# Two squared-ReLU layers on one core: seven block products for eight in the up-projection of 12 of 16 column groups, and weight sums formed by adding DMA transfers

## The chip, the core and the metric

One core of one Trainium2 chip runs the whole program. The metric is device time in microseconds (us), from the start to the end of one execution; the time of the kernel before is the median of three runs. The program is one launch, and all arithmetic is on the core. TensorE is called PE here, VectorE DVE, ScalarE ACT, GpSimd POOL and SyncE SP.

## The reference, cut to what matters

A trunk of two residual layers over 512 tokens of width 1024. Layer 0 mixes tokens by chunked softmax attention, layer 1 by a recurrent block; each is followed by the same kind of dense layer, and only these two dense layers ("MLP 0" and "MLP 1") are changed:

```python
def sq_relu_mlp(h, w1, w2):
    z = jax.nn.relu(jnp.einsum('bsd,df->bsf', h, w1))     # w1: 1024 x 4096
    return jnp.einsum('bsf,fd->bsd', z * z, w2)           # w2: 4096 x 1024
...
        h = h + sq_relu_mlp(rmsnorm(h, norm_mlp[layer]), mlp_w1[layer], mlp_w2[layer])
```

Inputs and output are float32. The RMS norm's per-token factor commutes with relu up to a square, so the kernel feeds `h * gain` into the up-projection and multiplies the squared per-token factor into the down-projection's result.

## The kernel before

**Three matmuls for one product.** Every fp32 operand X is split into a rounded part XH (type fp32r) and a rest XL = X - XH. `mm3` (L217) computes each product as WH·XH + WH·XL + WL·XH, three PE instructions into one PSUM bank. Activations are split once (ACT copies, DVE subtracts); weights are split as they arrive.

**Weights.** `plan` is a list of weight units of 512 KB (128 partitions x 1024 fp32), in the order in which PE uses them. `fetch` (L101) takes the next unit: SP issues its load, ACT casts the high part (L141), DVE subtracts to get the low part (L144). Raw tiles are `wr` (three buffers) or, for the down-projection, the eight tiles `b`; split tiles come from `wsp` (five pairs `wh`, `wl`) and in the MLPs from `wx` too (two more). `want` (L153) hands the next unit to PE after calling `prefetch`, which keeps `state["ahead"]` units fetched: five in the MLPs. The order in which the code emits instructions isn't quite the order in which each queue holds them: a planner of the framework orders each engine's and each DMA queue's instructions by when it expects them to be ready.

**An MLP** (`mlp`, L611) runs in four rounds p over 1024 of the 4096 hidden columns, with the model's width cut into eight blocks of 128 rows.

- *Up-projection*: `up(p, j)` (L649) computes 128 hidden columns for all 512 tokens: 8 row blocks x 3 = 24 matmuls with a 128x128 weight block loaded and 512 tokens moving. ACT applies relu (L656) and square (L657) from PSUM into the tile `a`. Eight units a round: a *group* of four units makes 512 hidden columns, two groups a round, 16 groups in the two MLPs.
- *Down-projection*: `round_(p)` (L669) cuts the 1024 x 512 activations and the 1024 x 1024 block of w2 into 2 x 2 blocks and forms the product with seven block products for eight (the Winograd form of Strassen's algorithm). The sums of activation blocks s1 to s4 (L687 and L731 to L734) are made by DVE, and so are the sums of weight blocks t1 to t4: `V.tensor_sub` in `fetch` (L139), in place in the tiles `b`. Each block product (`product`, L697) takes two weight units and 24 matmuls of 512 moving columns; `read` (L642) adds a PSUM bank, times the per-token factor, into the result.
- The first four up units of round p+1 stand between the block products of round p (`ahead`, L710), the other four open round p+1.
- In round 0 of an MLP, `turn` (L626) transposes the residual by DVE and 32 small DMAs, and `squares` forms the norm's sums.

PSUM holds four banks for up units (`mm`) and four for `X` and `Y` (`at`). GpSimd issues no DMA in this kernel.

The plan of one round in the kernel before, p < 3:

```python
for j in range(4, 8):
    up_(p, j)                       # after the last: "11", two halves
for n, kind in enumerate(("21", "t1", "22", "t2", "t3", "t4"), 1):
    ...                             # two halves each
    if p < 3 and 2 <= n <= 5:
        up_(p + 1, n - 2)
```

Of the kernel before, what the change touches and what calls it, by code (L numbers as in the profile page):

```python
# [15 lines left out]
P = 128  # L16
T = 512
# [23 lines left out]
def trunk(ctx: ExitStack, tc: tile.TileContext, xT, cols, gfin, win, wqkv, wo, rwin, rga, rgx, rwo, w1, w2, out):  # L41
# [4 lines left out]
    wraw = ctx.enter_context(tc.tile_pool(name="wraw", bufs=3))  # L46
# [13 lines left out]
    hT, hT2 = [], []  # L60


    def residual(name):
        both = [per.tile([P, 4, T], F32, name=f"{name}{i}", tag=f"hx{i}") for i in range(2)]
        hT[:] = [both[k // 4][:, k % 4] for k in range(KT)]
        hT2[:] = [both[k // 2][:, 2 * (k % 2) : 2 * (k % 2) + 2] for k in range(4)]
# [9 lines left out]
    rq = per.tile([P, 4], F32, name="rq")  # L76
    fs = per.tile([P, 8], F32, name="fs")
# [20 lines left out]
    state = {"next": 0, "ready": [], "ahead": 4, "stop": None, "more": None, "end": 0, "units": 0}  # L98
    raws, start_ = {}, []

    def fetch():  # L101
        i = state["next"]
        state["next"] += 1
        kind, nk, srcs = plan[i]
        pool = wsp
        if state["more"] is not None and i < state["end"]:
            pool = state["more"] if state["units"] % 7 >= 5 else wsp
            state["units"] += 1
        H = pool.tile([P, 1024], F32R, name=f"wh{i}", tag="wh")
        L = pool.tile([P, 1024], F32R, name=f"wl{i}", tag="wl")  # L110
        n = 1024
        if kind == "plain":
            n = nk * sum(src.shape[1] for src in srcs)
            raw = wraw.tile([P, 1024], F32, name=f"wr{i}", tag="wr")
            rv = raw[:, :n].rearrange("p (k c) -> p k c", k=nk)
            c0 = 0
            for n_, src in enumerate(srcs):
                w = src.shape[1]
                queue = nc.scalar if i == 0 and n_ else nc.sync
                queue.dma_start(rv[:, :, c0 : c0 + w], src.rearrange("(k p) c -> p k c", p=P))  # L120
                c0 += w
        else:
            half, nk = nk, 2
            if kind == "11" and half == 0:
                for name, src in zip(("11", "21", "12", "22"), srcs):
                    both = state["raw"].tile([P, 2, 1024], F32, name=f"b{name}_{i}", tag=f"b{name}")
                    for h in range(2):
                        raws[name, h] = both[:, h]
                        nc.sync.dma_start(
                            raws[name, h].rearrange("p (k c) -> p k c", k=2),  # L130
                            src[h * U : (h + 1) * U].rearrange("(k p) c -> p k c", p=P),
                        )

            at_, x, y = {
                "t1": ("12", "12", "11"), "t2": ("22", "22", "12"), "t3": ("11", "22", "11"), "t4": ("21", "21", "22"),
            }.get(kind, (kind, None, None))
            raw = raws[at_, half]
            if x:
                V.tensor_sub(raw, raws[x, half], raws[y, half])  # L139
# [40 lines left out]
    def add_mlp(layer):  # L180
# [5 lines left out]
        for j in range(4):  # L186
            up_(0, j)
        for p in range(4):
            srcs = [
                w2[layer][(2 * p + k) * T : (2 * p + k + 1) * T, c * T : (c + 1) * T]  # L190
                for k, c in ((0, 0), (1, 0), (0, 1), (1, 1))
            ]
            for j in range(4, 8):
                up_(p, j)
                if j == (5 if p == 3 else 7):
                    plan.extend(("11", half, srcs) for half in range(2))
            for n, kind in enumerate(("21", "t1", "22", "t2", "t3", "t4"), 1):
                for half in range(2):
                    plan.append((kind, half, srcs))
                if p < 3 and 2 <= n <= 5:  # L200
                    up_(p + 1, n - 2)
# [30 lines left out]
    class Norm:  # L232
# [8 lines left out]
        def square(self, k):  # L241
            if self.acc is None:
                self.both = wk.tile([P, 2, T], F32, name=f"{self.name}acc", tag="nn")
# [38 lines left out]
        def spread(self):  # L282
# [3 lines left out]
            r = wk.tile([P, 4, 4, 32], F32, name=f"{self.name}r", tag="nn")  # L286
# [9 lines left out]
    with ExitStack() as actx:  # L296
        ab = actx.enter_context(tc.tile_pool(name="ab", bufs=1))
# [313 lines left out]
    def mlp(ly, norm):  # L611
        with ExitStack() as mctx:
            sr, zp, dp = (mctx.enter_context(tc.tile_pool(name=f"{n}{ly}", bufs=1)) for n in ("sr", "z", "d"))
            wx = mctx.enter_context(tc.tile_pool(name=f"wx{ly}", bufs=2))
            end = starts[ly + 1] if ly + 1 < len(starts) else None
            state.update(raw=sr, more=wx, end=starts[ly] + 4 * 22, units=0, ahead=5, stop=end + 4 if end else None)
            xs = [(hnH[k], hnL[k]) for k in range(KT)]
            res = dp.tile([P, 4, 2, T], F32, name=f"d{ly}", tag="d")
            dt = {(t, c): res[:, t, c] for t in range(4) for c in range(2)}

# [21 lines left out]
            def read(acc, t, c):  # L642
                d, r = dt[t, c], rq[:, t : t + 1]
# [5 lines left out]
            def up(p, j):  # L649
                if j % 4 == 0:  # L650
                    a[p, j // 4] = zp.tile([P, 2, 4, U], F32, name=f"a{ly}{p}{j}", tag=f"a{j // 4}")
# [3 lines left out]
                c = a[p, j // 4][:, :, j % 4, :]  # L655
                S.activation(c, acc.rearrange("p (h c) -> p h c", h=2), AF.Relu)  # L656
                S.activation(c, c, AF.Square)  # L657
                if (p, j) == (0, 0):
                    turn()
                if (p, j) == (0, 5):  # L660
# [3 lines left out]
                if (p, j) == (0, 6):  # L664
                    V.tensor_add(rq, fs[:, 0:8:2], fs[:, 1:8:2])
                    V.tensor_scalar(rq, rq, 1.0 / D, EPS, ALU.mult, ALU.add)
                    V.reciprocal(rq, rq)

            def round_(p):  # L669
                A, low, raw = {}, {}, {}  # L670

                def room(n, kind, tag):
                    return (wk if tag == "nn" else zp).tile([P, 4, U], kind, name=f"{tag}{n}{ly}{p}", tag=tag)

                def place(n, h, l):
                    low[n] = (room(n, F32R, h), room(n, F32R, l))

                def split(n, ks=slice(0, 4)):
                    H, L = low[n]
                    S.copy(H[:, ks], raw[n][:, ks])  # L680
                    V.tensor_sub(L[:, ks], raw[n][:, ks], f(H[:, ks]))

                first, second = a[p, 0], None
                raw["11"], raw["s1"] = first[:, 0], first[:, 1]
                for n, tag in (("s3", "c"), ("s2", "f"), ("s4", "g")):
                    raw[n] = room(n, F32, tag)
                ins = V.tensor_sub(raw["s3"], raw["11"], raw["s1"])  # L687
                if (ly, p) == (0, 1):
                    constants(ins)
                place("11", "h0", "l")  # L690
                split("11")
                place("12", "h1", "nn")
                Y, X = ([atp(f"{b}{ly}{p}{t}") for t in range(2)] for b in "yx")
                Z = [mmp(f"z{ly}{p}{t}") for t in range(2)]
# [15 lines left out]
                def ahead(j):  # L710
                    if p < 3:
                        up(p + 1, j)


                def step(name, bank, fresh, t0, c):
                    apart = p == 3 and name != "12"
                    if not apart:
                        product(name, bank, fresh)
                    for t in range(2):
                        if apart:  # L720
                            product(name, bank, fresh, ts=(t,))
                        read(bank[t], t0 + t, c)

                chunks = {5: slice(0, 2), 7: slice(2, 4)} if p < 3 else {5: slice(0, 2), 6: slice(2, 3), 7: slice(3, 4)}
                for j in range(4, 8):
                    up(p, j)
                    raw["12"], raw["22"] = a[p, 1][:, 0], a[p, 1][:, 1]
                    if j in chunks:
                        ks = chunks[j]
                        r = {n: raw[n][:, ks] for n in raw}  # L730
                        V.tensor_sub(r["s2"], r["22"], r["s3"])  # L731
                        V.tensor_sub(r["s4"], r["12"], r["s2"])
                        split("12", ks)
                        V.tensor_add(r["s1"], r["s1"], r["22"])  # L734

                    if j == (5 if p == 3 else 7):
                        step("11", X, True, 0, 0)


                place("s1", "h0", "l")  # L740
                split("s1")
                step("12", Z, True, 0, 0)
                place("s4", "h1", "nn")
                split("s4")
                if p == 3:
                    state["ahead"] = 3
                step("s1", Y, True, 2, 1)
                place("s2", "h2", "g")
                split("s2")
                place("s3", "h0", "f")  # L750
                split("s3")
                ahead(0)
                step("s4", Y, False, 0, 1)
                place("22", "h1", "c")
                split("22")
                ahead(1)
                step("s2", X, False, 0, 1)
                ahead(2)
                if p == 3:

                    (ends if ly else turns)(step, product, X)
                    return
                step("s3", X, False, 2, 1)
                ahead(3)
                step("22", X, False, 2, 0)

# [9 lines left out]
            def turns(step, product, X):  # L776
                banks = [atp(f"back{i}") for i in range(2)]
# [305 lines left out]
```

## Time and profile before

| | |
|---|---|
| median of 3 runs | 1053.45 us (1053.26 to 1053.67) |
| profiled execution, device time | 1053.21 us |
| its span in the trace | 1051.4 us |
| mean granted PE clock | 0.998 of full speed |
| MLP 0, MLP 1 in the span | about 245 to 572 us, about 719 to 1045 us |
| up-projection matmuls, both MLPs | 3 x 512, each with 512 moving columns |
| bytes moved by DMA | 115.71 MB |

Times in the profile are microseconds from the start of the span unless ns stands beside them. A row of the groups gives the line of the code, the engine, the operation, its output and inputs by name, the shape and the count, then the busy time in all and the mean ns of one. Matmul records overlap (one is shown as 390 ns long, while the next one starts earlier), so the cost of a matmul in a train is the distance between two starts. A row of windows gives, for a stretch of time, the busy time and the count of instructions of each engine (PE, PEld, DVE, ACT, POOL), the granted clock, the share of time in which the 16 DMA engines were busy, and GB/s.

### The profile page before, as it was taken

The numbers are of one execution on the slowest core, as the hardware profiler recorded it, in microseconds if no ns is written. First come the engines' busy times: TensorE is split into PE (matmuls) and PEld (weight loads), VectorE is DVE, ScalarE is ACT, GpSimd is POOL, SyncE is SP. The second block draws the span as 40 slices with busy tenths as digits, with TensorE's granted clock in tenths as the row PEclk, the third lists the DMA queues.
The fourth block names the chain that finished last, engine by engine and source line by source line (L and its number), as shares of the span: only waits on it lengthen the run. The fifth ranks groups of instructions, "written<-read, shape, count | busy, mean of one in ns | idle before, by whom it ended". The sixth has DMA issues, their size and how long they took to land.

```text
span 1051.4 us, 12857 instructions
## 1 busy us (share of the span) xinstructions
PE 1042.3 (99%) x4754; PEld 865.5 (82%) x4754; DVE 807.2 (77%) x1202; ACT 579.9 (55%) x890; POOL 8.4 (1%) x28
## 2 busy tenths in 40 slices
PE   9999999999999999999999999999999999999997
PEld 8888888888888888888888888888888888888886
DVE  7899779867496687487599888984596587487596
ACT  7667557645553454454456786544554454454454
POOL 1000000000000000000000000000000000000000
PEclk9999999999999999999999999999999999999999
DMA  8344353243536026126103312164536026125002
GB/s 280 103 133 129 81 172 109 65 156 103 178 101 205 15 84 201 36 80 192 49 1 110 111 60 88 56 213 124 182 100 204 17 83 202 37 81 180 1 1 80
DMA packets 133534, 115.71 MB, mean 110 GB/s; under 512 B 5344, under 2 KB 109792, under 8 KB 133472
## 3 DMA queue, kind: packets, MB, share of 16 engines
q1 hardware_dynamic: 132896, 114.18, 35.3%
q8 instruction: 37, 0.61, 0.2%
q10 hardware_dynamic: 576, 0.72, 0.2%
q14 instruction: 25, 0.20, 0.1%
HBM read 104.39 MB, written 2.10 MB: 101 GB/s over the span
## 4 chain that ended last, share of the span: by engine, by line
PE 97%; DVE 1%; ACT 1%; issue 0%; DMA 0%; POOL 0%; ACTq 0%; POOLq 0%
PE u L220 11%; PE u L218 11%; PE u L219 11%; PE x L218 6%; PE x L220 6%; PE x L219 6%; PE y L218 3%; PE y L220 3%; PE y L219 3%; PE x L444 2%; PE wo L218 1%; PE wo L219 1%; PE v L218 1%; PE ro L219 1%; PE ro L218 1%; PE v L220 1%
## 5 line engine op out<-in xcount | busy, mean ns | idle before, releaser
L144 DVE TENSOR_TENSOR wl<-wr,wh 128x1024 fp32r<-128x1024 f32 (+1 forms) x122 | 146.4, 1202 | 77.2 <-ACT wh L141 77.0
L141 ACT CAST wh<-b 128x1024 fp32r<-128x1024 f32 x112 | 117.7, 1051 | 158.5 <-PE u L219 105.8
L141 ACT CAST wh<-wr 128x1024 fp32r<-128x1024 f32 (+1 forms) x121 | 125.6, 1040 | 137.7 <-PE u L219 60.4
L218 PE MATMUL u<-hnH,wh 128*128 128x512 f32 x512 | 199.4, 390 | 0.0
L220 PE MATMUL u<-hnH,wl 128*128 128x512 f32 x512 | 199.4, 390 | 0.0
L219 PE MATMUL u<-hnL,wh 128*128 128x512 f32 x512 | 199.4, 390 | 0.0
L144 DVE TENSOR_TENSOR wl<-b,wh 128x1024 fp32r<-128x1024 f32 x112 | 136.7, 1222 | 79.3 <-ACT wh L141 79.1
L219 PEld LDWEIGHTS u<-hnL,wh 128*128 128x128 f32 x512 | 96.2, 188 | 20.0
L220 PEld LDWEIGHTS u<-hnH,wl 128*128 128x128 f32 x512 | 96.2, 188 | 19.9
L218 PEld LDWEIGHTS u<-hnH,wh 128*128 128x128 f32 x512 | 96.2, 188 | 19.8
L139 DVE TENSOR_TENSOR b<-b,b 128x1024 f32<-128x1024 f32 x64 | 76.5, 1220 | 0.2
L656 ACT ACTIVATE a<-u 128x512 f32<-128x512 f32 x64 | 37.8, 591 | 32.2 <-PE u L220 32.2
L218 PE MATMUL x<-wh,h 128*128 128x512 f32 (+1 forms) x132 | 50.9, 386 | 0.6 <-DVE d L853 0.6
L219 PE MATMUL x<-wl,h 128*128 128x512 f32 (+1 forms) x132 | 50.7, 384 | 0.0
L644 DVE SCALAR_TENSOR_TENSOR d<-x,rq,d 128x512 f32<-128x512 f32 x63 | 44.9, 744 | 2.3 <-PE x L220 2.3
L657 ACT ACTIVATE a<-a 128x512 f32<-128x512 f32 x64 | 40.5, 633 | 1.8
L424 ACT ACTIVATE p<-p,mx 128x128 f32<-128x128 f32 (+1 forms) x64 | 35.2, 552 | 7.0 <-DVE mx L421 6.8
L680 ACT CAST h<-a 128x1024 fp32r<-128x1024 f32 (+2 forms) x34 | 27.2, 799 | 7.6 <-PE y L219 6.7
L417 DVE CUSTOM_DVE_ANT_0 p<-s,bias 128x128 f32<-128x128 f32 (+1 forms) x64 | 27.7, 485 | 4.2 <-PE s L414 4.2
L448 ACT CAST pH<-x 128x512 fp32r<-128x512 f32 (+1 forms) x48 | 21.8, 516 | 16.1 <-PE x L444 16.1
L218 PEld LDWEIGHTS x<-wh,h 128*128 128x128 f32 x132 | 24.8, 188 | 5.5 <-DVE d L853 0.8
L219 PEld LDWEIGHTS x<-wl,h 128*128 128x128 f32 x132 | 24.8, 188 | 4.8
(340 smaller groups left out, 2276.8 us busy)
## 6 DMA issues: line engine op xcount, KB each, us to landing
wr<-in_w SPq DMA_DIRECT2D x64, 512.0 KB, 4.0
b<-in_w SPq DMA_DIRECT2D x64, 512.0 KB, 5.5
wr<-in_wqkv SPq DMA_DIRECT2D x20, 512.0 KB, 3.9
wr<-in_rwin SPq DMA_DIRECT2D x16, 512.0 KB, 3.4
wr<-in_wo SPq DMA_DIRECT2D x8, 512.0 KB, 3.7
d<-turned SPq DMA_DIRECT2D x64, 64.0 KB, 2.0
wr<-in_rwo SPq DMA_DIRECT2D x8, 512.0 KB, 3.6
x<-in_xT SPq DMA_DIRECT2D x8, 256.0 KB, 3.7
```

The lines of the kernel that those rows point to most:

```text
L139: V.tensor_sub(raw, raws[x, half], raws[y, half])
L141: S.copy(H[:, :n], raw[:, :n])
L144: low = V.tensor_sub(L[:, :n], raw[:, :n], f(H[:, :n]))
L218: PE.matmul(acc, WH, XH, start=start, stop=False, skip_group_check=more)
L219: PE.matmul(acc, WH, XL, start=False, stop=False, skip_group_check=more)
L220: PE.matmul(acc, WL, XH, start=False, stop=stop, skip_group_check=more)
L417: V.tensor_tensor_reduce(out=pt[:, seg[t] : seg[t] + n], in0=sc[t], in1=b[:, h % 4, T - n :], scale=1.0, scalar=-3.0e38, op0=ALU.add, op1= ...
L424: S.activation(pt[:, seg[t] : seg[t] + n], pt[:, seg[t] : seg[t] + n], AF.Exp, bias=mx[:, t : t + 1], accum_out=sm[:, t : t + 1],)
L644: V.scalar_tensor_tensor(d, acc, r, d, ALU.mult, ALU.add)
L656: S.activation(c, acc.rearrange("p (h c) -> p h c", h=2), AF.Relu)
L657: S.activation(c, c, AF.Square)
L680: S.copy(H[:, ks], raw[n][:, ks])
```

## The change

- **Up-projection of 12 groups.** In rounds 1 to 3 (six groups in each MLP) a group's 1024 x 512 block of w1 and the activations are cut into 2 x 2 blocks: 512 rows each way, 256 hidden columns, and 256 tokens (a *token half*). Seven block products make the group (`group`), each from one weight unit of 512 x 256 with 256 tokens moving: 2 x 4 x 3 = 24 matmuls of 256 columns. Round 0 keeps `up`.
- The sums of the activation blocks are made once per MLP in round 0, in place in the residual's tiles: `scaled` multiplies the gain in (ACT), `right` forms four sums (DVE), `right_split` splits them (ACT and DVE).
- Between the products, ACT copies the first bank to SBUF (`c1`), and DVE adds it to others (`u`, `v`, and two adds in `out_`); signs go into the relu's scale and into `nrq`, the negated per-token factor.
- **Weight sums.** No DVE subtraction of weights is left in `fetch`. A sum is formed by a DMA issued from GpSimd that adds into the raw tile (`accum_op=ALU.add`), from DRAM or from another raw tile; block 11 of w2 is loaded over by block 22 after its split. Per group: five plain loads (`upper`) and four adding transfers. Per round's down-projection: eight plain loads (`blocks`), two plain reloads, and eight adding transfers.
- **Order.** The units of a round p >= 1 are: the seven of group (p, 1), back to back; then the fourteen of the down-projection in the order 11, t1, 22, 21, t2, t3, t4 (two halves each), with one unit of group (p+1, 0) after every pair. `ahead` is 3 in the MLPs.
- **Memory.** `wx` is gone, `wraw` keeps three tiles with tags of their own, the activations get seven shared tiles (`take`, `give`), and GpSimd's scratch for DMA descriptors goes from 1024 to 2048.

The diff, cut to its core:

```diff
+    def blocks(srcs):
+        for name, src in srcs.items():
+            both = state["raw"].tile([P, 2, 1024], F32, name=f"b{name}_{state['next']}", tag=f"b{name}")
+            for h in range(2):
+                raws[name, h] = both[:, h]
+                nc.sync.dma_start(two(raws[name, h]), rows(src, h))
+        for h in range(2):
+            G.dma_start(two(raws["12", h]), rows(srcs["11"], h), accum_op=ALU.add)
+
+    def upper(srcs):
+        i = state["next"]
+        for n, tag, src in (("11", "wr0", "11"), ("s1", 0, "21"), ("s2", "wr1", "11"), ("12", "wr2", "12"), ("22", 1, "22")):
+            raws["u" + n] = state["kept"][:, tag] if n in ("s1", "22") else wraw.tile([P, 1024], F32, name=f"u{n}_{i}", tag=tag)
+            nc.sync.dma_start(raws["u" + n].rearrange("p (k c) -> p k c", k=4), srcs[src].rearrange("(k p) c -> p k c", p=P))
+        raws["us3"], raws["us4"] = raws["u11"], raws["u12"]
+        G.dma_start(raws["us1"].rearrange("p (k c) -> p k c", k=4), srcs["22"].rearrange("(k p) c -> p k c", p=P), accum_op=ALU.add)
+        G.dma_start(raws["us2"], raws["us1"], accum_op=ALU.add)
 
     def fetch():
...
-            if x:
-                V.tensor_sub(raw, raws[x, half], raws[y, half])
...
+        if kind == "11":
+            nc.sync.dma_start(two(raw), rows(srcs["22"], half))
+            G.dma_start(two(raw), rows(srcs["12"], half), accum_op=ALU.add)
+        elif kind == "22":
+            G.dma_start(raw, raws["12", half], accum_op=ALU.add)
+        elif kind == "21":
+            G.dma_start(raw, raws["22", half], accum_op=ALU.add)
+        elif kind == "u11":
+            G.dma_start(raw.rearrange("p (k c) -> p k c", k=4), srcs["21"].rearrange("(k p) c -> p k c", p=P), accum_op=ALU.add)
+        elif kind == "u12":
+            G.dma_start(raw, raws["us2"], accum_op=ALU.add)
...
+            plan.extend(("u" + n, 4, srcs) for n in ("11", "s2", "12", "s1", "s3", "s4", "22"))
...
+            if p:
+                add_group(p, 1)
+            tail = [plan.pop()] if p == 3 else []
+            if p < 3:
+                add_group(p + 1, 0)
+                tail = plan[-7:]
+                del plan[-7:]
+            for kind in ("11", "t1", "22", "21", "t2", "t3", "t4"):
+                plan.extend((kind, half, srcs) for half in range(2))
+                plan.extend(tail[:1])
+                del tail[:1]
...
+            def group(p, g):
+                def piece(bank, op, fresh):
+                    WH, WL = want(1)
+                    for i in range(2):
+                        for k, (XH, XL) in enumerate(operand(op)):
+                            mm3(bank[:, i * U : (i + 1) * U], WH(k, PAIR[i]), WL(k, PAIR[i]), XH, XL, fresh and k == 0 and i == 0, k == 3, True)
+
+                def out_(i, j, bank, more, sign):
+                    if i == j:
+                        a[p, g, j] = take(F32, f"a{p}{g}{j}")
+                    c = a[p, g, j][:, 2 * i : 2 * i + 2].rearrange("p i c -> p (i c)")
+                    if more is not None:
+                        V.tensor_add(c, bank, more)
+                        bank = c
+                    S.activation(c, bank, AF.Relu, scale=sign)
+                    S.activation(c, c, AF.Square)
+
+                b1 = mmp(f"m1{ly}{p}{g}")
+                piece(b1, "11", True)
+                c1 = wk.tile([P, T], F32, name=f"c1{ly}{p}{g}", tag="nsq", bufs=2)
+                S.copy(c1, b1)
+                yield
+                b6 = mmp(f"m6{ly}{p}{g}")
+                piece(b6, "r2", True)
+                u = wk.tile([P, T], F32, name=f"u{ly}{p}{g}", tag="nsq", bufs=2)
+                V.tensor_add(u, b6, c1)
+                yield
+                piece(b1, "21", False)
+                out_(0, 0, b1, None, 1.0)
+                yield
...
+                piece(b6, "r4", False)
+                out_(1, 0, b6, c1, -1.0)
+                yield
```

More of the change, by code (lines that the diff above doesn't have):

```diff
@@ L124, in fetch @@
             if kind == "11" and half == 0:
[L125 to L137, printed above, removed]
-            if x:
-                V.tensor_sub(raw, raws[x, half], raws[y, half])
+                blocks(srcs)
+            raw = raws[{"t1": "12", "t2": "22", "t3": "11", "t4": "21"}.get(kind, kind), half]
+        state["next"] += 1
         if i:
@@ L667, in up @@
                     V.reciprocal(rq, rq)
-            def round_(p):
[L670 to L692, printed above, removed]
+                    V.tensor_scalar(nrq, rq, -1.0, None, ALU.mult)
@@ new lines, in round_ @@
+                split("s1", "h1")
+                if p == 3:
+                    step("11", X, True, 0, 0)
+                if p:
+                    next(here)
+                sums(True)
+                if p < 3:
+                    step("11", X, True, 0, 0)
+                then = group(p + 1, 0) if p < 3 else iter(range(7))
+                next(then)
+                split("s4", "h2")
+                step("s1", Y, True, 2, 1)
+                next(then)
+                split("12", "h0")
```

239 lines of the change are left out of this document (156 added, 83 removed).

## The prediction

> **What bounds the kernel now.** I read the page's busy times, the chain that ended last, the PE timeline for the cost of a matmul, then windows of the MLPs, the groups, and the DMA views.
>
> ```profile
> PE 1042.3 (99%) x4754; PEld 865.5 (82%) x4754; DVE 807.2 (77%) x1202; ACT 579.9 (55%) x890; POOL 8.4 (1%) x28
> PE 97%; DVE 1%; ACT 1%; issue 0%; DMA 0%; POOL 0%; ACTq 0%; POOLq 0%
> PE u L220 11%; PE u L218 11%; PE u L219 11%; PE x L218 6%; PE x L220 6%; PE x L219 6%; PE y L218 3%; PE y L220 3%; PE y L219 3%; PE x L444 2%; PE wo L218 1%; PE wo L219 1%; PE v L218 1%; PE ro L219 1%; PE ro L218 1%; PE v L220 1%
> ```
>
> The chain is PE for 97%, a third of it (3 x 11%) the up-projection `u`. PE "busy" overlaps records, so the price of a matmul is read from starts in a train: nineteen rows of 512 moving columns, then twelve of 256 (with the first two weight loads).
>
> ```profile
> 1024.82 0.39 PE L220 MATMUL y<-wh,nns 128*128 128x512 f32 x1
> ...
> 1028.90 0.39 PE L220 MATMUL y<-wh,nns 128*128 128x512 f32 x1
> ...
> 1041.82 0.28 PE L218 MATMUL x<-wh,h 128*128 128x256 f32 x1
> 1041.82 0.19 PEld L219 LDWEIGHTS x<-wl,h 128*128 128x128 f32 x1
> ...
> 1041.94 0.19 PEld L220 LDWEIGHTS x<-wh,c 128*128 128x128 f32 x1
> ...
> 1043.13 0.28 PE L220 MATMUL x<-wh,c 128*128 128x256 f32 x1
> ```
>
> 18 steps in 4.08 us: **226.7 ns** for 512 columns. 11 steps in 1.31 us: **119.1 ns** for 256, with a new weight block each time: loads recorded as 0.19 us start 0.12 us apart, so a load hides behind half-length matmuls too. Half the columns cost 5.8 ns more than half the time.
>
> ```profile
> 325.00:405.00 80.00, 80.00 (x355) 66.30 (x354) 60.24 (x90) 38.39 (x46) 0.00 (x0) 1.00 0.32 100
> 405.00:485.00 80.00, 80.00 (x355) 66.30 (x354) 55.72 (x58) 38.09 (x45) 0.00 (x0) 1.00 0.33 102
> ```
>
> Two windows of MLP 0: 355 matmuls x 0.2267 = 80.5 us in 80 us. PE runs gapless at a granted clock of 1.00; DVE is at 70 to 75%, ACT at 48%, DMA at a third. Only fewer PE columns, or a stall that isn't there now, can move the time.
>
> **The change, part by part.**
>
> *PE.* A group of `u` is now 4 units x 24 = 96 matmuls of 512: 96 x 0.2267 = 21.76 us. As seven products it is 7 x 24 = 168 of 256: 168 x 0.1191 = 20.01 us. Saved 1.75 us a group, **21.0 us** for twelve. It would be nothing at 21.76/168 = 129.5 ns a matmul.
>
> [...]
>
> *DVE and ACT in a full round* (p = 1, 2: 28 weight units; PE 14 x 12 x 0.2267 + 14 x 24 x 0.1191 = 38.1 + 40.0 = 78.1 us).
>
> ```profile
> L144 DVE TENSOR_TENSOR wl<-b,wh 128x1024 fp32r<-128x1024 f32 x112 | 136.7, 1222 | 79.3 <-ACT wh L141 79.1
> L141 ACT CAST wh<-b 128x1024 fp32r<-128x1024 f32 x112 | 117.7, 1051 | 158.5 <-PE u L219 105.8
> L139 DVE TENSOR_TENSOR b<-b,b 128x1024 f32<-128x1024 f32 x64 | 76.5, 1220 | 0.2
> L656 ACT ACTIVATE a<-u 128x512 f32<-128x512 f32 x64 | 37.8, 591 | 32.2 <-PE u L220 32.2
> L644 DVE SCALAR_TENSOR_TENSOR d<-x,rq,d 128x512 f32<-128x512 f32 x63 | 44.9, 744 | 2.3 <-PE x L220 2.3
> L657 ACT ACTIVATE a<-a 128x512 f32<-128x512 f32 x64 | 40.5, 633 | 1.8
> L681 DVE TENSOR_TENSOR l<-a,h 128x1024 fp32r<-128x1024 f32 x8 | 9.8, 1224 | 6.1 <-ACT h L680 6.1
> L920 DVE TENSOR_TENSOR xp<-xb,n1r 128x512 f32<-128x512 f32 x8 | 5.5, 687 | 1.3 <-PE xb L220 1.1
> ```
>
> DVE: 28 weight splits x 1.22, 11 activation sums and splits x 1.22, 14 reads x 0.744, 8 adds from PSUM (as L920) x 0.69 = 34.2 + 13.4 + 10.4 + 5.5 = 63.5 us, 81% of 78.1. The removed 64 sums x 1.22 = 78 us (L139) are what makes room; DVE wasn't the bound, so they earn nothing themselves. ACT: 28 x 1.05 + 7 x 1.0 + 16 x 0.61 + 2 x 0.6 = 47 us, 60%. Tightest are the seven units of group (p, 1) in a row: in 20 us DVE has 7 + 6 operations of 1.22 and 4 of 0.69, 18.6 us, 93% (a train of such operations overlaps a little in the trace). Round 0 gains on DVE 8 x 1.22 = 9.8 us, on ACT 8 gains, 4 casts and the halved relus, some 12 us, in 8 x 24 x 0.2267 = 43.5 us of PE; the first window of the MLP (quoted below) has 22 and 34 us free of 80. I cost these at nothing, except small waits where the 93% stretch uses its cover up: 0 to 2 us for each of six, **4 us** taken.
>
> *DMA.* The trace has no adding transfer and no DMA from GpSimd, so its price is bounded by plain ones.
>
> ```profile
> b<-in_w SPq DMA_DIRECT2D x64, 512.0 KB, 5.5
> wr<-in_rwin SPq DMA_DIRECT2D x16, 512.0 KB, 3.4
> ```
>
> ```profile
> 405.00:410.00 5.00, 5.00 (x24) 4.14 (x23) 4.42 (x6) 2.11 (x2) 0.00 (x0) 1.00 1.06 362
> 410.00:415.00 5.00, 5.00 (x24) 4.15 (x23) 1.88 (x3) 1.73 (x3) 0.00 (x0) 1.00 0.94 325
> 245.00:325.00 80.00, 80.00 (x354) 66.26 (x354) 58.23 (x70) 45.86 (x67) 0.00 (x0) 1.00 0.43 127
> ```
>
> The stretch of block loads moves (362 + 325)/2 = 344 GB/s at a full share: 524 KB take 1.52 us of all 16 engines. An adding transfer reads two operands for one written: between 1.5 us (nothing extra) and 3.0 us (twice). A full round has 20 plain loads and 16 adding ones: 30.4 + (24 to 48) = 54 to 78 us of 78.1. I take the middle, 66 us (85%): no row is nearer to either end.
>
> From issue to landing an adding transfer takes at least the 3.4 us of an uncrowded load, and at most, by estimate, the crowded 5.5 plus a second data time of 1.5 and 1 us for GpSimd's part: 8. I take 5.5, the crowded row, because these come in bunches. The longest chain is load, add into us1, add into us2. Its buffers come free when us3 of the group before is split, and us2's own turn is eight units later in either position: 8 x 2.8 = 22 us, plus up to 5 us of lead (three units fetched ahead, 8.3 us, less 2.3 of casting and subtracting and some queueing). 5.5 + 2 x 5.5 = 16.5 us fits; it no longer fits above (22 + 5 - 5.5)/2 = 10.8 us each. u12 + us2 has three units, 8.5 us, plus the lead: about the same. So the loads' waits cost nothing at my price. What covers them is that lead; without it each us over 8.3 would be paid twice a group.
>
> The new wait stands at ACT's head: the cast of us2 waits for a DMA, behind it the `c1` copy, the activation casts and relus, and on DVE the low part; PE then lives on three units. On SP the reload of block 11 waits for DVE's split, with the next group's loads behind it by the code. But queues aren't in the code's order: it emits eight `b` loads in a row (L125 to L132), and SP issued them mixed with `wr`:
>
> ```profile
> 386.56 0.88 SPq L129 DMA_DIRECT2D b<-in_w  x2
> 392.42 0.37 SPq L120 DMA_DIRECT2D wr<-in_w  x1
> 400.60 0.37 SPq L129 DMA_DIRECT2D b<-in_w  x1
> 401.68 0.37 SPq L120 DMA_DIRECT2D wr<-in_w  x1
> 402.10 6.42 SPq L129 DMA_DIRECT2D b<-in_w  x5
> ```
>
> The planner puts a load where its buffer comes free, so I let the upper loads pass the reloads, as they may on GpSimd too.
>
> *Sum.* Profiled 1053.21 us: span 1051.4 and 1.8 around it. Span 1051.4 - 21.0 + 4 = 1034.4; with 1.8, 1036.2. The median lies 0.24 above the profiled run: **1036.5 us**.
>
> **The rivals.**
>
> *A (slower): the DMA engines become the bound.* From 3.0 us of all engines per adding transfer a full round's transfers no longer fit behind its matmuls; at 3.3 us (30.4 + 52.8 = 83.2, 5.1 over in each of four full rounds) the gain is gone. At 3.6 us: 88.0, 9.9 us over, 39.6 in all: 1036.5 + 39.6 = **1076**. For it: the upper bound already fills the round, and latency grows with the queue (5.5 against 3.4). Against: shares today are 0.32 to 0.43, and copies within SBUF move longer rows. A sign would be idle PE with ACT casts waiting for POOL's DMAs.
> [...]
>
> *B: the weights come late in part.* us2, or DVE's 93% stretch, stalls PE by about 1.1 us a group beyond my 4: 12 x 1.1 = 13: **1049**. For it: three units of lead in place of five. Against: 5.5 us is far under 10.8.
>
> *C: 256-column matmuls run faster in long trains*, at half the 512-column step: 113.4 ns, 168 x 0.1134 = 19.05 us a group, saved 2.71 x 12 = 32.5 us, 11.5 more than my 21.0: **1025**. For it: half the columns. Against: the eleven steps above, mean 119.1 ns. [...]
>
> *D: it evens out.* Stalls eat all of the 21 us: within 0.2% (2.1 us, what a measurement of this kernel can tell), 1051.3 to 1055.6.
>
> **How the numbers follow.** Forecast 0.60 (1032.5, no stall, to 1043); B 0.17 (1043 to 1051.3); C 0.03; D 0.04; A 0.16. Faster: 0.60 + 0.17 + 0.03 = 0.80; same 0.04; slower 0.16. The range leaves out A and D: from 1031.5 (the floor 1032.4 less about 1 us for the removed DVE work) to 1051.5. Both unknown costs, landing time and DMA share, lie in it up to their upper bounds.
>
> **What would show it.** Right: matmuls of 256 columns 119 ns apart; no L139 group; PE idle under 5 us in all; DVE near 80% in the middle rounds; DMA share there 0.7 to 1.0; GpSimd's transfers landing in 4 to 8 us. Wrong: a step of 130 ns or more; idle PE after `wl`, whose ACT cast waited for GpSimd's queue (A, B), or after DVE adds of `u` and `v` (B); adding transfers landing after 11 us or later.

## The result, and the profile after

| | time, median of 4 runs | lowest to highest | span of the profiled execution | granted PE clock |
|---|---|---|---|---|
| before | 1053.39 us | 1053.26 to 1053.67 | 1051.4 us | 0.998 |
| after | 1084.92 us | 1082.89 to 1087.62 | 1085.8 us | 0.982 |

The change makes the kernel slower: the ratio after to before is 1.0301 (95% interval 1.0276 to 1.0325). The forecast was 1036.5 us, faster.

From the page after, the busy times, the clock by slices, and the two large DMA queues (SP's, then GpSimd's; packets, MB, share of 16 engines):

```profile
PE 1035.0 (95%) x5618; PEld 896.1 (83%) x5618; DVE 832.3 (77%) x1212; ACT 638.5 (59%) x984; POOL 129.1 (12%) x140
PEclk9999999999979999999999999999979899999999
q1 hardware_dynamic: 119008, 128.87, 37.4%
q0 software_dynamic: 29440, 58.73, 31.2%
```

PE was 99% busy before; now it idles some 50 us for 9, and the clock dips in three slices (each is 27 us). Landmarks of the two traces put the loss there. The first `u` matmul stands at 244.58 us before and 244.70 after, that of MLP 1 at 717.91 and 733.62, and the last matmul starts at 1045.4 and 1079.0. From MLP 0's start to MLP 1's it takes 15.6 us longer, in MLP 1 17.9, elsewhere about 1. PE's waits over the whole span, after (us in total, times, longest), show which:

```profile
PE m L254 <- ACT wh L156: 22.4, 2, 12.2
PE m L254 <- ACT c L777: 11.6, 3, 5.2
PE m L256 <- DVE wl L159: 2.3, 4, 0.8
```

`m` is a bank of the seven products. Two waits for a weight cast are 22.4 us, one in each MLP. They stand in the first group that takes seven products, as the windows of MLP 0 show (us, PE busy, granted clock, DMA share, GB/s):

```profile
290.00:300.00 10.00, 9.97 (x56) 1.00 1.11 278
300.00:310.00 10.00, 2.55 (x12) 0.76 0.77 136
310.00:320.00 10.00, 4.80 (x25) 0.55 0.45 87
360.00:370.00 10.00, 7.83 (x64) 1.00 0.57 100
```

A second pair of waits, 5.2 us each for ACT's `c1` copy, near 370 and 860, stands one group later. ACT's rows show what held the copy:

```profile
363.14 1.05 ACT L156 CAST wh<-us 128x1024 fp32r<-128x1024 f32 x1 [11.39 <-DMA us<-kept]
...
372.94 0.58 ACT L777 COPY c<-m 128x512 f32<-128x512 f32 x1
```

It is us2 again, now the second group's own: its cast waited 11.4 us for the adding transfer, and the copy stands behind that cast on ACT's queue, as the prediction had said of the new wait. Rounds further on run gapless, at a full DMA share:

```profile
400.00:440.00 40.00, 40.00 (x235) 35.47 (x234) 31.34 (x34) 19.86 (x21) 9.46 (x10) 1.00 1.03 246
440.00:480.00 40.00, 40.00 (x280) 37.51 (x279) 31.98 (x33) 26.81 (x33) 8.66 (x8) 1.00 0.98 230
480.00:520.00 40.00, 40.00 (x235) 35.46 (x234) 30.12 (x32) 19.04 (x21) 9.49 (x9) 1.00 1.05 250
```

So the wait is followed back from the cast that came late. From the timelines after, SP's queue, GpSimd's, and ACT (start, us, engine, line, operation, output and input, idle time before it):

```profile
271.10 2.57 SPq L114 DMA_DIRECT2D b<-in_w  x4
281.61 2.35 SPq L163 DMA_DIRECT2D b<-in_w  x2
284.00 0.55 SPq L122 DMA_DIRECT2D u<-in_w  x1
284.59 0.53 SPq L122 DMA_DIRECT2D kept<-in_w  x1
```

```profile
288.88 1.20 POOL L164 DMA_DIRECT2D b<-in_w  x1 [8.58 <-DMA b<-in_w]
290.31 1.23 POOL L164 DMA_DIRECT2D b<-in_w  x1 [0.23 <-issue]
298.21 1.31 POOL L124 DMA_DIRECT2D kept<-in_w  x1 [6.68 <-issue]
...
305.94 1.47 POOL L125 DMA_DIRECT2D us<-kept  x1
```

```profile
313.63 1.04 ACT L156 CAST wh<-us 128x1024 fp32r<-128x1024 f32 x1 [13.98 <-DMA us<-kept]
```

The first group's upper loads (L122) are issued at 284, behind the reloads of block 11 (L163), which waited for that block's splits. us1's add goes out at 298.2, us2's at 305.9, and us2's cast starts at 313.6: **29.0 us** from us1's load (284.59) to the cast, where the prediction had 16.5. That is 13.6 until us1's add goes out, then 7.7 and 7.7.

### The profile page after: what moved, and what is told of

Read it like the earlier page. It is cut to its first block, busy times and chain, and to the rows that moved or that the text cites. A ratio compares the mean times of both kernels' runs of the same rounds, so it can differ in the third digit from the quotient of the medians.

```text
span 1085.8 us, 15138 instructions
## 1 busy us (share of the span) xinstructions
PE 1035.0 (95%) x5618; PEld 896.1 (83%) x5618; DVE 832.3 (77%) x1212; ACT 638.5 (59%) x984; POOL 129.1 (12%) x140
## 3 DMA queue, kind: packets, MB, share of 16 engines
q1 hardware_dynamic: 119008, 128.87, 37.4%
q0 software_dynamic: 29440, 58.73, 31.2%
## 5 line engine op out<-in xcount | busy, mean ns | idle before, releaser
L254 PE MATMUL m<-rH,wh 128*128 128x256 f32 x384 | 110.2, 287 | 22.4 <-ACT wh L156 22.4
L256 PE MATMUL m<-rH,wl 128*128 128x256 f32 x384 | 110.1, 287 | 2.3 <-DVE wl L159 2.3
L255 PE MATMUL m<-rL,wh 128*128 128x256 f32 x384 | 109.7, 286 | 0.0
L159 DVE TENSOR_TENSOR wl<-wr,wh 128x1024 fp32r<-128x1024 f32 (+1 forms) x74 | 87.7, 1189 | 17.5 <-ACT wh L156 17.0
L254 PEld LDWEIGHTS m<-rH,wh 128*128 128x128 f32 x384 | 74.8, 195 | 24.3 <-ACT wh L156 23.4
L254 PE MATMUL m<-hnH,wh 128*128 128x256 f32 x288 | 83.7, 291 | 11.6 <-ACT c L777 11.6
L255 PE MATMUL m<-hnL,wh 128*128 128x256 f32 x288 | 83.2, 289 | 0.0
L256 PE MATMUL m<-hnH,wl 128*128 128x256 f32 x288 | 83.1, 289 | 0.0
L256 PEld LDWEIGHTS m<-rH,wl 128*128 128x128 f32 x384 | 74.7, 194 | 3.3 <-DVE wl L159 3.3
L255 PEld LDWEIGHTS m<-rL,wh 128*128 128x128 f32 x384 | 74.9, 195 | 0.9
```

What stands on the lines that cost most here:

```text
L159: low = V.tensor_sub(L[:, :n], raw[:, :n], f(H[:, :n]))
L254: PE.matmul(acc, WH, XH, start=start, stop=False, skip_group_check=more)
L255: PE.matmul(acc, WH, XL, start=False, stop=False, skip_group_check=more)
L256: PE.matmul(acc, WL, XH, start=False, stop=stop, skip_group_check=more)
```

## The experiments

One theory and two rivals were written ahead of the first runs: that the first group's chain (load, add into us1, add into us2) is late, having no lead; against it, that the DMA engines are full everywhere, or that GpSimd's descriptor ring (`dynamic_dma_scratch_size`, 2048 in the change) holds the chain up. All ratios are to the kernel before, with 95% intervals.

**1. Ten groups.** The first group of each MLP goes back to four up units.

```diff
+PLAIN = [(1, 0)]
...
         def add_group(p, g):
+            if (p, g) in PLAIN:
+                for j in range(4):
+                    up_(p, 4 * g + j)
+                return
...
```

> Ten groups for twelve: the first group of each MLP, (1,0), which stands between the products of round 0, goes back to four up units of 512 tokens. Theory (late first chain): PE lost its time at one place of each MLP, where the first group's us2 is still being added together when its turn comes (12.2 us idle at 302 us), and once more in group (1,1) as an echo (5.2 us at 362 us). Without group (1,0) nothing is urgent in round 0, group (1,1) has a whole round's lead, both stalls go, and the time is 1053.4 - 10 x 1.75 + 2 to 7 = 1038 to 1043 us. Rival (the DMA engines are full everywhere): two groups fewer take away 2 x (5 x 1.65 + 4 x 3.0) = 40 us of DMA time of some 640 in the MLPs, the stall moves to the next group, and the time stays above 1065 us. Rival (GpSimd's descriptor ring holds too little): as the second, above 1065 us.

Measured: 1045.53 us, ratio 0.9913 (0.9892 to 0.9933). The long waits are gone, PE's longest for a weight or `c1` is 0.2 us, and the second group has no stall though its sums are still made by adding transfers: with no group ahead of it to hold the buffers, its first `kept` load is out early enough for GpSimd's add to wait 8.5 us for its landing between 285 and 310 us, where the changed kernel issues that load at 328.0. So its stall was the first group's echo. That speaks against full engines as the cause. The time lies 2.5 us above what was expected; runs 6 and 8 show most of that.

**2. A larger descriptor ring.**

```diff
-dynamic_dma_scratch_size=2048
+dynamic_dma_scratch_size=3840
```

> The kernel after with GpSimd's descriptor scratch at 3840 for 2048. Theory (late first chain): GpSimd's waits before the add into us1 end when the plain load under it lands, not when the ring has room; at most 3 us per stalled group: 1076 to 1086 us. Rival (ring): the adds overlap instead of going one by one, us2 comes some 7 us sooner at both stalls: under 1072 us. Rival (DMA engines full): no change, within 0.3%.

Measured: 1078.78 us, ratio 1.0237 (1.0221 to 1.0253), 6 us under the changed kernel. GpSimd in the first group:

```profile
292.97 1.30 POOL L124 DMA_DIRECT2D kept<-in_w  x1 [1.56 <-DMA kept<-in_w]
...
305.46 0.90 POOL L125 DMA_DIRECT2D us<-kept  x1 [9.87 <-DMA kept<-in_w]
```

us1's add goes out 5 us earlier, without the wait put down to "issue"; then us2's add waits 9.9 us for us1's to land, and is where it was. The ring holds a little, 6 us in all; it isn't the main cause.

**3. Reloads behind the upper loads.** The reload and add of block 11 are emitted after the next unit's loads.

```diff
         if kind == "11":
-            nc.sync.dma_start(two(raw), rows(srcs["22"], half))
-            G.dma_start(two(raw), rows(srcs["12"], half), accum_op=ALU.add)
+            state["late"].append((raw, srcs, half))
+        if kind == "us2" or kind == "t1":
...
```

> The kernel after, in which the two reloads of block 11 and the two adds on them (needed ten units later) are emitted behind the next group's five loads and two adds instead of ahead of them. Theory (late first chain): 2 x 1.65 + 2 x 3.0 = 9 us of DMA time leave the front of us2's chain, the first stall shrinks from 12 us to about 4 and its echo with it, the cold clock behind them too: 1052 to 1070 us. Rival (DMA engines full): the same transfers in another order, 1080 us or more. Rival (ring): the adds into us1 and us2 meet an emptier ring, also faster; the run of the larger ring tells it apart.

Measured: 1076.67 us, ratio 1.0212 (1.0189 to 1.0235), a miss. From its timelines of SP, GpSimd and ACT:

```profile
274.10 0.53 SPq L122 DMA_DIRECT2D kept<-in_w  x1
```

```profile
290.74 1.32 POOL L124 DMA_DIRECT2D kept<-in_w  x1 [10.43 <-DMA kept<-in_w]
```

```profile
308.67 1.04 ACT L156 CAST wh<-us 128x1024 fp32r<-128x1024 f32 x1 [12.09 <-DMA us<-kept]
```

us1's load goes out 10.5 us earlier (274.10 for 284.59), us2's cast starts only 5.0 earlier. The chain is now 34.6 us long: half of the head start is lost among the transfers around it (DMA share 1.11 from 280 to 290 us). PE still waits 7.5 us for us2's cast in MLP 0, and 11.2 us in MLP 1 for an activation cast, in a stretch in which ACT does nothing from 780 to 790.

**4. us1 and us2 by VectorE, in every group.** 24 adding transfers become 24 DVE adds.

```diff
-        G.dma_start(raws["us1"].rearrange("p (k c) -> p k c", k=4), srcs["22"].rearrange("(k p) c -> p k c", p=P), accum_op=ALU.add)
-        G.dma_start(raws["us2"], raws["us1"], accum_op=ALU.add)
...
+            if kind == "us2":
+                V.tensor_add(raws["us1"], raws["us1"], raws["u22"])
+                V.tensor_add(raw, raw, raws["us1"])
```

> The kernel after, in which us1 = 21 + 22 and us2 = 11 + us1 of a group are two DVE adds just ahead of us2's split (block 22 lies in kept anyway); two of the four adding transfers of a group are gone. Theory (late first chain): the chain behind the loads shrinks from two adding transfers (7 to 10 us each) to 2 x 1.22 us of DVE, both stalls go; DVE's own load in a full round rises from 81% to 63.5 + 4.9 = 68.4 of 78.1 us (88%) and may cost 1 to 3 us in each of the six rounds of an MLP pair: 1038 to 1050 us. Rival (DMA engines full): 24 adds x 3.0 = 72 us of DMA time less out of some 640, a gain in proportion, stalls stay in the first group: 1055 to 1070 us.

Measured: 1079.96 us, ratio 1.0242 (1.0222 to 1.0263), a miss. The chain has only loads for transfers, and is still late; DVE, in the first group:

```profile
301.80 1.23 DVE L148 TENSOR_TENSOR kept<-kept 128x1024 f32<-128x1024 f32 x1 [1.80 <-DMA kept<-in_w]
```

The last of its two plain loads has only then landed. PE also has six waits for `c1`, 13.2 us in all and 3.3 at most, spread over the rounds. So a crowd in front of the chain had to be told apart from the chain, and the first group from the later ones. The next runs do that.

**5. No adds at all.** Every adding transfer is left out; the products are of unsummed blocks.

> All adding transfers are left out (the weight sums are not formed, so the products are of unsummed blocks); every plain load, every wait on a load, all products and casts stay. Theory (the first group's sums are late because the chain load, add, add has no lead there and its transfers stand in a crowd of adds): without adds nothing is late, the 12 groups keep their saving of some 1.5 us each, 1034 to 1042 us, no wait of TensorE for a weight cast over 2 us. Rival (the narrower matmuls or the new order of products cost more than counted): 1053 us or more, with a gapless TensorE.

Measured: 1037.96 us, ratio 0.9854 (0.9834 to 0.9873). PE's longest wait in an MLP is 0.7 us. This is the floor of the 12 groups: the products bring 15.5 us, and the adding transfers cost 47 (1084.92 - 1037.96). None of that is lost in a full round: from the last product of group (2, 0) to the same product a round later PE takes 78.4 us here and 78.4 in the changed kernel (444.98 to 523.35), where the DMA engines are full.

**6. No group of seven.** Run 1's edit for all six groups of each MLP; the down-projection's sums stay with the adds.

> None of the 16 groups of the up-projection takes seven products (all are up units of 512 columns again); the weight sums of the down-projection are still made by adding transfers. Theory (the chain of the upper sums in the first group is what costs): 1050 to 1056 us, no stall over 3 us. Rival (the adding transfers of the down-projection cost time by themselves, by filling the DMA engines or by coming late): 1060 us or more.

Measured: 1061.86 us, ratio 1.0080 (1.0063 to 1.0097). The time lies in the rival's range, but the stalls the rival needs aren't there: no wait in an MLP is over 1.1 us, yet a full round is 0.7 us longer than before (82.3 for 81.6). Part of this is the experiment's own: its four up units leave the first two places between the down products empty, so two `y` products stand nearly together, and one waits for the other's reads. What the down-projection's adds cost alone can't be read from it.

**7. The first round's sums by VectorE.** Eight DVE operations in place of eight adds and two reloads per MLP, in round 0 only.

```diff
+            if id(srcs) in byhand and kind[0] == "t":
+                if kind == "t3":
+                    V.tensor_sub(raw, raws["22", half], raw)
+                else:
+                    V.tensor_add(raw, raw, raws[{"t1": "11", "t2": "12", "t4": "22"}[kind], half])
...
+            if p == 0:
+                byhand.add(id(srcs))
...
```

> 12 groups of seven products as in the changed kernel; only the first down-projection round of each MLP has its weight sums made by VectorE (8 operations of about 1.2 us for 8 adds and 2 reloads of 512 KB). Theory in the form that the crowd of the first round's adds makes the first chain late: TensorE waits under 6 us for the first group in each MLP instead of 18, the echo in the next group goes too, 1040 to 1052 us. Theory in the form that the chain itself, started behind the block loads, is too long even alone: 1060 to 1072 us. Rival (DMA engines full in the later rounds): 1070 us or more, with stalls spread over all rounds.

Measured: 1053.42 us, ratio 0.9997 (0.9987 to 1.0007): 31.5 us from 16 adds and four reloads. Its SP, GpSimd, ACT and PE:

```profile
275.13 0.51 SPq L125 DMA_DIRECT2D kept<-in_w  x1
```

```profile
286.74 1.45 POOL L127 DMA_DIRECT2D kept<-in_w  x1 [117.41 <-DVE nrq L767]
...
293.95 1.48 POOL L128 DMA_DIRECT2D us<-kept  x1
```

```profile
301.62 1.05 ACT L164 CAST wh<-us 128x1024 fp32r<-128x1024 f32 x1 [6.02 <-DMA us<-kept]
```

```profile
302.86 0.28 PE L266 MATMUL m<-rH,wh 128*128 128x256 f32 x1
```

Without that crowd the chain is done at 301.6, 12 us earlier: 9.5 us because us1's load goes out at 275.13 for 284.59, with no reload ahead of it, and 2.5 because the chain is shorter, 26.5 us for 29.0. It is still a little late. PE takes up us2's product at 302.86 and waits 0.7 us for the low part; behind the cast DVE and ACT run late, and PE waits 2.5 us for a read of `y` in MLP 0, 3.2 for an activation cast in MLP 1, and 2.2 in the echo.

**8. The same, with ten groups** (runs 1 and 7 together).

> Ten groups of seven products (the first group of each MLP back in up units) and the first down-projection round's weight sums by VectorE. Theory (what is left in the run with ten groups is the first round's own crowd of adds): 1036 to 1042 us, the stall of 2.3 us at 290 to 300 us gone. Rival (the rest is not from that crowd): 1044 to 1048 us, as with ten groups alone.

Measured: 1043.59 us, ratio 0.9908 (0.9894 to 0.9923). No wait in an MLP is over 0.7 us. With all stalls gone, ten groups should stand two groups' gain above the floor: 1037.96 + 2 x 15.5/12 = 1040.5. It is 3 us more, above the range expected: the crowd was 2 us of run 1's gap. Of the 3, some 1.4 can be run 6's order, whose 0.7 us a round stands here in one round of each MLP (an estimate); the rest is open.

**9. First round and first group by VectorE.** Run 7, and run 4's two adds for group (1, 0) alone.

```diff
+            if (p, g) in ((1, 0),):
+                upper_byhand.add(id(srcs))
...
+        if id(srcs) in upper_byhand:
+            return
```

> 12 groups; the first down-projection round's weight sums by VectorE as in the run before, and in the first group of each MLP the two chained upper sums (us1, us2) by VectorE too, so that of its chain load, add, add only the load is a transfer. Theory (what is left there is the first chain, 275 to 302 us, 3 us too long, with the clock drop and the echo behind it): 1039 to 1045 us, first-group waits of TensorE under 1 us. Rival (VectorE, which now waits for a load in its order, passes the wait on): 1050 us or more, waits of TensorE for VectorE or for casts at 290 to 310 us.

Measured: **1039.82 us**, ratio 0.9876 (0.9859 to 0.9892): faster than both kernels, and 1.9 us above the floor. DVE and ACT in the first group:

```profile
292.71 1.22 DVE L155 TENSOR_TENSOR kept<-kept 128x1024 f32<-128x1024 f32 x1
...
297.44 1.22 DVE L156 TENSOR_TENSOR us<-us,kept 128x1024 f32<-128x1024 f32 x1
```

```profile
298.68 1.05 ACT L169 CAST wh<-us 128x1024 fp32r<-128x1024 f32 x1 [0.43 <-DVE us L156]
```

No bracket stands behind the two adds: the loads had landed, and DVE came to them in its turn. The echo at 360 us is gone too, and the 92 adding transfers that are left make PE wait no more than 0.3 us in an MLP.

**10. The second group by VectorE too.** `((1, 0),)` becomes `((1, 0), (1, 1))`.

> As the run with the first group's us1 and us2 by VectorE, and the second group's (the one behind it) too. Theory (the second group has its stall only as an echo of the first): the same time within 2 us as with the first group alone. Rival (the second group's chain is late by itself, since its loads also stand in the crowd of the rounds behind): faster by 3 us or more than with the first group alone.

Measured: 1052.57 us, ratio 0.9997 (0.9979 to 1.0014): both expectations were wrong, it is 12.7 us slower than run 9. A new wait of 5.2 us, `m` for `c1`, stands at 433 to 439, and smaller new ones add another 5. The long one belongs to group (2, 1): as in the changed kernel's echo, the copy stands behind us2's cast, which waited 11.6 us for its adding transfer. GpSimd issued that group's two adds late; run 9, then run 10:

```profile
400.40 1.31 POOL L129 DMA_DIRECT2D kept<-in_w  x1 [2.87 <-DVE wl L172]
411.76 0.89 POOL L130 DMA_DIRECT2D us<-kept  x1 [10.05 <-DMA kept<-in_w]
```

```profile
411.13 1.30 POOL L129 DMA_DIRECT2D kept<-in_w  x1 [7.69 <-DVE a L788]
421.43 0.90 POOL L130 DMA_DIRECT2D us<-kept  x1 [9.00 <-DMA kept<-in_w]
```

Already group (2, 0) has its pair of `kept` loads later, issued on SP by 351.8 for 346.6. One reading is that a sum made in DVE's turn keeps its sources' buffers longer, and the groups behind lose their lead; the rows fit it, but no run takes it apart.

**11. All down-projection sums by VectorE**, run 7's edit for all rounds.

> 12 groups; the weight sums of all eight down-projection rounds by VectorE (64 operations more of about 1.2 us), those of the up-projection by adding transfers. Theory (the time is lost in the first group alone): 1050 to 1056 us, as with the first round alone by VectorE, with the same waits at 300 and 350 us. Rival 1 (the DMA engines, at about full share in all the later rounds, cost time there too): under 1047 us. Rival 2 (VectorE, 77% busy and some 9% more by this, becomes late itself): over 1058 us.

Measured: 1056.01 us, ratio 1.0025 (1.0014 to 1.0036), 2.6 us over run 7. The later rounds' DMA share falls, and PE gains nothing by it (us, PE busy, clock, share, GB/s):

```profile
400.00:440.00 40.00, 40.00 (x268) 1.00 0.88 226
440.00:480.00 40.00, 40.00 (x250) 1.00 0.54 125
```

It was gapless there with the engines full (the windows of the changed kernel above) and it is gapless with them half full. That speaks a second time against full engines in the later rounds.

**12. The first group alone by VectorE**, the first round's sums by adds again. It fills the square.

> 12 groups; us1 and us2 of the first group of each MLP by VectorE, the first down-projection round's weight sums by adding transfers again. Theory (two causes add up: the chain load, add, add in the first group, and the crowd of the first round's adds and reloads in front of it): the loads still land late, some 10 us of waits a MLP stay, 1055 to 1070 us, between the changed kernel and the run with both by VectorE. Rival (the chain alone was the cause): 1039 to 1045 us, as with both. Rival (the crowd alone was the cause): 1075 to 1087 us, as the changed kernel.

Measured: 1066.99 us, ratio 1.0125 (1.0105 to 1.0145).

| first round's sums | first group by adds | first group by VectorE |
|---|---|---|
| by adding transfers | 1084.92 (the change) | 1066.99 (run 12) |
| by VectorE | 1053.42 (run 7) | 1039.82 (run 9) |

The crowd is worth 31.5 or 27.2 us, the chain 17.9 or 13.6: two causes, 45.1 us together, and neither alone explains the loss. What in the crowd costs most isn't taken apart: adds and reloads leave together in run 7, and run 3, which only moves the reloads, gives 8 us. In run 12 the loads go out on SP as in the changed kernel (us1's at 285.44) and land as late as in run 4:

```profile
302.71 1.23 DVE L155 TENSOR_TENSOR kept<-kept 128x1024 f32<-128x1024 f32 x1 [1.79 <-DMA kept<-in_w]
```

## Why the prediction was wrong

**PE: right.** A train of the seven products after, first and last of 36 rows:

```profile
535.79 0.28 PE L255 MATMUL m<-rL,wh 128*128 128x256 f32 x1
...
540.00 0.28 PE L254 MATMUL m<-rH,wh 128*128 128x256 f32 x1
```

35 steps in 4.21 us are 120.3 ns for the 119.1 taken; by it twelve groups save 12 x (21.76 - 168 x 0.1203) = 18.6 us for 21.0. Run 5 has 15.5. Most of the difference is a pair of waits of 0.7 us in the last round of each MLP, where the down products stand back to back and wait for the split of activation sums: 2.9 us in all, which the kernel before doesn't have. 17 was forecast, after 4 us for small waits. Without adds the forecast would have missed by 1.5 us; that the 4 us came near is luck, since they were put at another place, the 93% stretch of DVE. Rival C is out.

**DVE and ACT: right in size.** DVE is 75 to 80% busy in the middle rounds (30.12 to 31.98 of 40 us, above; 81% forecast), ACT 48 to 67% (60%). They cost little in the changed kernel: a full round is as long there as in run 5.

**DMA engine time: at its upper bound, taken too low.** GpSimd's queue is 31.2% of 1085.8 us for 112 adds, **3.02 us** of all 16 engines each, the upper bound (3.0); I took the middle. Rival A started at that value. A full round is 20 x 1.65 (a plain one, last section) + 16 x 3.02 = 81 us of transfers beside 78 of matmuls, but its mechanism, a round that doesn't fit, didn't come: full rounds are gapless at a share of 1.0. Its time, 1076, was close by luck: the loss lies in one stretch, round 0 and the first group behind it.

**The chain's length: this step failed.** "5.5 + 2 x 5.5 = 16.5 us fits": the changed kernel's first chain has 13.6 + 7.7 + 7.7 = 29.0, and run 7's, without the crowd, 11.6 + 7.2 + 7.7 = 26.5. After, by kind of add (KB each, median us to landing):

```profile
b<-b POOLq DMA_DIRECT2D x32, 512.0 KB, 7.0
kept<-in_w POOLq DMA_DIRECT2D x12, 512.0 KB, 9.6
us<-kept POOLq DMA_DIRECT2D x12, 512.0 KB, 7.6
u<-us POOLq DMA_DIRECT2D x12, 512.0 KB, 5.9
```

5.9 to 9.6 us for the 5.5 taken. The 9.6 is above the 8 estimated as the most; the 1 us for GpSimd's part in it had no row of the kernel before behind it, and GpSimd's issues after take 0.86 us (`b<-b`, L166) to 1.47 (`us<-kept`, L125). Each landing is within the 10.8 I allowed, but that limit left 5.5 for the load, and us1's add went out 13.6 us after it.

**The lead: this step failed too.** "Its buffers come free when us3 of the group before is split, and us2's own turn is eight units later in either position": so 22 + 5 us of lead, in every group. The first group of each MLP has no group before it. PE wanted us2's product at 302.5 (314.73 less its wait of 12.18, below), 18 us after us1's load went out, not 27. Run 7, with no reload ahead of that load, has 27.7 (275.13 to 302.86), but with 2.3 us of casting and subtracting behind its 26.5 that isn't enough either. Where there is a group before, the chain cost next to nothing in rounds 2 and 3, but not by the sizes of the prediction. SP, ACT and PE of group (2, 1) after:

```profile
411.48 1.81 SPq L122 DMA_DIRECT2D kept<-in_w  x1
```

```profile
442.63 1.05 ACT L156 CAST wh<-us 128x1024 fp32r<-128x1024 f32 x1 [4.74 <-DMA us<-kept]
```

```profile
450.67 0.28 PE L254 MATMUL m<-rH,wh 128*128 128x256 f32 x1
```

The chain is 31.2 us there and the lead 39.2: both were taken too short by 12 to 15 us, and that the steady groups came out covered is luck.

**The queue: this step failed as well.** "I let the upper loads pass the reloads": on SP the reloads went out at 281.61 and the loads behind them at 284.00. Without the reloads us1's load goes out 9.5 us earlier (run 7). Letting it pass them (run 3) gives only 8 us of time, since other transfers then stretch the chain to 34.6. I priced the transfers per full round, and never round 0's: four of its eight block loads (271.10), two reloads and four of its eight adds go out between 271 and 291, in front of the first group's chain or beside it.

**Rival B** came nearest as a mechanism: us2 stalls PE. But it was to be about 1.1 us in each of twelve groups; it was 12.2 and 10.2 us in the first group of the two MLPs, 5.2 in the second, and no more than 1.3 anywhere else. **The clock** was in no step. After the 12.2 us wait of the changed kernel:

```profile
314.73 0.58 PE L254 MATMUL m<-rH,wh 128*128 128x256 f32 x1 [12.18 <-ACT wh L156]
...
318.71 0.37 PE L256 MATMUL m<-rH,wl 128*128 128x256 f32 x1
318.93 0.28 PE L254 MATMUL m<-rH,wh 128*128 128x256 f32 x1
```

Until 318.7 the matmuls start some 0.21 us apart, then 0.12: 15 steps take 4.2 us in place of 1.8, 0.5 of it a wait for the low part. The granted clock of the windows (0.76, 0.55) says the same. The same steps stand behind the other three long waits: 15 of them near 370 (373.57 to 376.94), and in MLP 1 23 behind the wait of 10.2 us (801.27 to 807.12) and 27 near 860 (862.68 to 868.55). At 0.1203 us a step, and without the waits for the low part, the four stretches take 1.9, 1.6, 2.6 and 2.6 us more, 8.7 in all. With the 36 us of waits named at the start that is 45 of the 47 us above the floor; the rest isn't accounted for. How long a wait has to be for this, the rows don't show: in run 7 the clock is 1.00 in the window of the 2.5 us wait and in the one behind it, but 0.83 in the window of the 3.2 us wait and in the one behind the 2.2 us wait of the echo.

## What to carry to other kernels

A lead worked out for the steady state has to be worked out again for the first turn of each loop, where no turn before frees the buffers early (18 us here for 39 in the steady state) and where the prologue's own transfers stand in the same queues: write down for the first group when each load can be issued, what is ahead of it on its queue, and what else lands then. In this kernel the adding transfers were best replaced on the critical path alone: moving the first group's two sums and the first round's to VectorE took it from 3.0% slower to 1.2% faster than the kernel before, while moving the second group's two as well lost that gain again (run 10). A stall of TensorE of 5 us or more was dearer than its length, by 1.6 to 2.6 us in the changed kernel.

## What the runs showed of the hardware

- An adding transfer of 512 KB took 1.8 times the engine time of a plain one: 3.02 us of all 16 engines in the changed kernel, and again 29.8% of 1046.6 us for 104 of them, 3.00, in run 1, and 25.0% of 1074.9 us for 88, 3.05, in run 4. SP's plain transfers are 37.4% of 1085.8 us for 128.87 MB, 1.65 us per 524 KB.
- PE ran gapless for 120 us while the DMA share stood at 0.98 to 1.05: its full round took 78.4 us, as in run 5, where no add was made. Full engines by themselves cost nothing there, where each transfer was issued early enough.
- A plain 512 KB load of `wr` landed in a median of 4.2 us in the changed kernel; the two `kept` loads of run 12's first group, in the crowd (DMA share 1.05 and 1.11 from 280 to 300 us), took a median of 11.3 us.
